# Latent attention in a two-layer encoder: shuffled rope halves, half-bank query sums, and scores of two heads in one chain

## The chip, the cores and the metric

The kernel runs on one core of one Trainium2 chip. The metric is device time in microseconds. The kernel before took 2838.72 us, the median of three runs (2837.63 to 2839.24). One core has a matrix engine (TensorE, PE in the views, with PEld for its weight loads), a vector engine (DVE), a scalar engine (ACT), GpSimd (POOL) and a queue that issues most transfers (SP). Each engine takes its instructions in the order in which they were written into its queue. PE writes its sums to PSUM, here eight banks of 128 partitions by 512 f32.

## The reference

The trunk has two layers, 256 tokens and 2048 features. Each layer mixes two attentions, then a gated feed-forward and a gated per-layer embedding follow. Cut to what matters here:

```
h  = rmsnorm(x, g_mix[i]);  z = h @ w_in[i]
dq, dk, dv, cq, ckv, kr, ga, gb = split(z)      # 8 heads of differential attention from dq, dk, dv
qf = (rmsnorm(cq) @ w_q_up[i]).reshape(b, s, 8, 128 + 64)
q_nope, q_rope = qf[..., :128], apply_rope(qf[..., 128:], cos_m, sin_m)
k_nope, v_mla  = split((rmsnorm(ckv) @ w_kv_up[i]).reshape(b, s, 8, 256), 2)
k_rope = apply_rope(kr)                         # one 64-wide rotary key for all 8 heads
scores = (q_nope . k_nope + q_rope . k_rope) * (128 + 64) ** -0.5
om     = softmax(scores) @ v_mla
m = sigmoid(ga) * (A @ w_branch_diff) + sigmoid(gb) * (om @ w_branch_mla);  x = x + m @ w_out[i]
```

apply_rope takes the two 32-wide halves x1, x2 of a 64-wide vector and gives [x1 c - x2 s, x2 c + x1 s].

## The kernel before

Activations lie feature by token: a tile is 128 features by 256 tokens. Every f32 operand of a product is cut into a high and a low part (`split`: ACT copies the high part, DVE subtracts it for the low one), and a product is high.high + high.low + low.high. Weights come by SP into `w` (four buffers), ACT makes `whi` and DVE makes `wlo` of each piece (three buffers each, lines 187 and 75). `product` and `pair` call `emit`: for each piece of 128 rows one matmul of `whi` with 512 columns (the high and low part of the activation side by side, L212) and one of `wlo` with the 256 high columns (L216). The two halves of the bank are then added by `joined`: ACT copies one half into `join`, DVE adds it to the other (`a<-mm,join`), into a scratch `a` that has four buffers. After that the bank is free. The pool `ps_mm` has four banks (`mm`, also `mmv` for the values), `ps_s` has two for scores (`S`), `ps_at` two for all else (`at`).

The order of each engine's queue is set by the framework's scheduler, which lays all instructions out on a modelled timeline; the program's order and the tile pools bound what it can do. A tile that takes a buffer over waits until all that used the buffer are done.

Per layer the stages follow each other so: values of the differential heads; the products for queries and keys of heads 0 to 7 (`queries_keys`), with `keys_up`, the narrow product of the rotary key and, at the end, `queries_up` laid beside the differential heads as filling (`beside`); the latent values (`vm`, L460 to L462 into `mmv`); the eight latent heads beside the 16 products of `gate(wga)`; the 16 products of `gate(wgb)`; the branch products, `w_out` and the feed-forward, which is most of the time.

Four things bear on the change. `queries_up(n)` makes two tiles of the 12 of `w_q_up`: n below 8 are the unrotated queries of heads n and n+1 (`qn`, written to `fa(n)`), n = 8 and 10 the rotated parts of four heads each (`qr`), which pass through `rotated`. `rotated` swaps the 32-wide halves by an f32 matmul with a permutation (`swap`, `swaps`, L367), multiplies by cosine and sine and splits the sum; for the rotary key it also copies the 64 rows to the other 64 (`halves`, L366) and fills two tiles `krs`, each zero on one half of its rows. `mla_weights(h)` makes one head's scores: two query blocks with six matmuls each, three of `qn` with `kn` and three of `qr` with one of `krs` over all 128 rows (L406); `exps` then takes the row maxima on DVE (L412) and the exponentials on ACT (L415). `mla_out(h)` transposes the weights and multiplies them with the values.

The tiles `fa0` to `fa7` have one buffer each. In a layer `fa(h)` first holds the key operand of differential head h, then its output `od[h]` (`diff_out`, L635), which `settle(0)` and `settle(4)` normalize four heads at a time: the squares' sums of the four heads go through `rsqrt` (eleven small DVE instructions, `rv`, `ry`, `ra`), the outputs are scaled (L81) and transposed (L647) into `ub` (ACT L251, DVE L78). `settle(4)` needs head 7. Only then can `fa(4)` to `fa(7)` take the latent queries of heads 4 to 7. The calls stand in the order

```python
            settle(0)
            for n in (8, 0, 2, 10):
                queries_up(n)
                yield
            settle(4)
            for n in (4, 6):
                queries_up(n)
```

Of the kernel before, what the change touches and what calls it, by code (L numbers as in the profile page):

```python
# [12 lines left out]
F32 = mybir.dt.float32  # L13
F32R = mybir.dt.float32r
# [5 lines left out]
P = 128  # L20
T = 256
# [32 lines left out]
def encoder(ctx, tc, x, p, positions, cols, lams, wq, wk, wv, wcq, wckv, wkr, wga, wgb,  # L54
# [16 lines left out]
    def bank(ps=ps_at, tag="at", name="at", shape=(P, 2 * T)):  # L71
        return ps.tile(list(shape), F32, tag=tag, name=name)

    def tt(o, a, b, op):
        return V.tensor_tensor(out=o, in0=a, in1=b, op=op)  # L75
# [43 lines left out]
    swap, swaps, halves = (rc[:, 4 + j * P : 4 + (j + 1) * P] for j in range(3))  # L119
    aside = [fa(j) for j in range(5)]  # L120
    posi = aside[0][:, 0, :].bitcast(I32)
    posf = aside[0][:, 1, :]
# [86 lines left out]
    def emit(acc, hi, lo, at, us, first, last, inside=None):  # L209
        for j, u in enumerate(us):  # L210
            s, start, stop = slice((at + j) * P, (at + j + 1) * P), first and j == 0, last and j == len(us) - 1
            lead = PE.matmul(acc, hi[:, s], u, start=start, stop=False)  # L212
# [27 lines left out]
    def joined(acc, o=None):  # L240
        t = scratch("join", 3)
        A.activation(t, acc[:, T:], AF.Copy)  # L242
        o = scratch("a", 4) if o is None else o
        tt(o, acc[:, :T], t, ALU.add)
        return o

    def split(u, src, gain=None):
        hi, lo = u[:, :T], u[:, T:]
        if gain is None:
            return A.activation(hi, src, AF.Copy), tt(lo, src, hi.bitcast(F32), ALU.subtract)  # L250
        return A.activation(hi, src, AF.Copy, scale=gain), stt(lo, src, gain, hi.bitcast(F32), ALU.mult, ALU.subtract)  # L251
# [104 lines left out]

    krs = [const.tile([P, 2 * T], F32R, name=f"kr{j}") for j in range(2)]
    for t in krs:  # L360
        nc.gpsimd.memset(t.bitcast(F32), 0.0)

    def rotated(a, c_, s_, o=None):
        r = bank()
        if o is None:
            PE.matmul(r[:, T:], halves, a, start=True, stop=True)  # L366
        PE.matmul(r[:, :T], swap if o is not None else swaps, a, start=True, stop=True)  # L367
        t = scratch("sh", 2)
        tt(t, r[:, :T], s_, ALU.mult)
        tt(a, a if o is not None else r[:, T:], c_, ALU.mult)  # L370
        tt(a, a, t, ALU.add)
        if o is None:
            for j, t in enumerate(krs):
                split(t[64 * j : 64 * j + 64], a[64 * j : 64 * j + 64])
        else:
            split(o, a)

# [20 lines left out]
    def scores(*maps):  # L398


        Ss = [bank(ps_s, "S", "S", (P, 2, T)) for _ in maps]
        for b in range(2):
            for j in range(len(maps[0])):
                for S, pairs in reversed(list(zip(Ss, maps))):
                    q, k = pairs[j]
                    PE.matmul(S[:, b, :], q[:, b * P : (b + 1) * P], k, start=j == 0, stop=j == len(pairs) - 1)  # L406
        return Ss
# [26 lines left out]

    def weights(tag="E", dt=F32):
        return tmp.tile([P, 2, T], dt, tag=tag, name=tag, bufs=2)

    last_exp = [None]
    ROPE16 = [(j + 8) if j < 8 else (j - 8) if j < 16 else j for j in range(32)]

    def values(src, us, load=None):
# [43 lines left out]
    for L in range(DEPTH):  # L485
# [64 lines left out]
                split(kn[-1], joined(acc))  # L550

        def queries_up(n):
            for acc in pair(w_q_up[L, n : n + 2], cq):
                if n < MH:
                    qn.append(operand(fa(len(qn), F32R)))
                    split(qn[-1], joined(acc))
                else:
                    if n > MH:
                        qr.append(operand(fc(len(qr) - 2, F32R)))
                    at = qr[len(qr) - 1] if n > MH else qr[ropes[0]]  # L560
                    rotated(joined(acc), cos_m, sin_m, at)
                    ropes[0] += 1

        ropes = [0]
# [102 lines left out]
        oms = ub[8:]  # L667
        todo = iter(range(NC))

        def mla_weights(h):  # L670
            E = weights()
            S, = scores(three(qn[h], kn[h]) + three(qr[h // 2], krs[h % 2]))
            r = exps(S, E, MLA_SCALE)
            for b in range(2):
                ts(E[:, b, :], E[:, b, :], r[:, b : b + 1], None, ALU.mult)
            return E

        def mla_out(h, W):
            v = head(vm, slice(None), h)
            vs = weights("E1", F32R)  # L680
            vh, vl = vs[:, :, :P], vs[:, :, P:]
            A.activation(vh, v, AF.Copy)
            tt(vl, v, vh.bitcast(F32), ALU.subtract)
            wh, wl = turned(W, True)
            yield
            o = bank()
            for kb in range(2):
                for j, (a, b) in enumerate(((vh, wh), (vh, wl), (vl, wh))):
                    PE.matmul(o[:, :T], a[:, kb, :], b[:, kb, :], start=kb + j == 0, stop=kb + j == 3)  # L689
# [196 lines left out]
        ("g_q_latent0", 4), ("g_q_latent1", 4), ("g_kv_latent0", 2), ("g_kv_latent1", 2), ("g_subln", 2)]  # L886


def rope_constants():


    c = np.zeros((P, 4 + 3 * P), np.float32)
    f32 = np.float32
    for base, dim in ((0, 16), (2, 64)):
        inv = f32(THETA) ** (-np.arange(0, dim, 2, dtype=f32) / f32(dim))
        for q in range(P):
            d = q % 64
            if d < dim:
                c[q, base] = inv[d % (dim // 2)]
                c[q, base + 1] = -1.0 if d < dim // 2 else 1.0  # L900
    for q in range(P):
        c[q, 4 + (q ^ 32)] = 1.0
        for m in (q, q ^ 64):
            c[q, 4 + P + (m ^ 32)] = 1.0
            c[q, 4 + 2 * P + m] = 1.0
    return c


# [18 lines left out]
def laid_out(a):  # L927
    a = {k: np.asarray(v) for k, v in a.items()}
    w_in = a["w_in"]
    cut = np.cumsum([0, 1024, 1024, 1024, QR, KVR, 64, DM, DM])  # L930
    z = [w_in[:, :, cut[j] : cut[j + 1]] for j in range(8)]
    up = a["w_q_up"].reshape(DEPTH, QR, MH, 192)
    kv = a["w_kv_up"].reshape(DEPTH, KVR, MH, 256)
    flat = lambda w: w.reshape(w.shape[0], w.shape[1], -1)
    named = {f"{n}{i}": a[n][i] for n in ("g_mix", "g_ffn", "g_ple", "g_q_latent", "g_kv_latent") for i in range(DEPTH)}
    named["g_final"] = a["g_final"]
    named["g_subln"] = a["g_subln"]
    return {
        "x": np.ascontiguousarray(a["x"][0].T.reshape(NC, P, T).transpose(1, 0, 2)),
        "p": np.ascontiguousarray(a["p"][:, 0].transpose(0, 2, 1).reshape(DEPTH, 2, P, T).transpose(0, 2, 1, 3)),  # L940
        "positions": np.ascontiguousarray(a["positions"]),
        "cols": np.ascontiguousarray(np.concatenate([columns(named[n]) for n, _ in COLS], axis=1)),
        "lams": np.ascontiguousarray(np.stack([a["lambda_q1"], a["lambda_q2"], a["lambda_k1"], a["lambda_k2"]], axis=1).reshape(1, -1)),
        "wq": tiles(z[0]), "wk": tiles(z[1]), "wv": wide(z[2]), "wcq": tiles(z[3]), "wckv": tiles(z[4]),
        "wkr": np.ascontiguousarray(z[5].reshape(DEPTH, NC, P, 64).transpose(0, 2, 1, 3)).reshape(DEPTH, P, NC * 64), "wga": tiles(z[6]), "wgb": tiles(z[7]),
        "w_q_up": tiles(np.concatenate([flat(up[..., :128]), flat(up[..., 128:])], axis=2)),
        "w_kn": tiles(flat(kv[..., :128])), "w_v": wide(flat(kv[..., 128:])),
        "w_bd": tiles(a["w_branch_diff"]), "w_bm": tiles(a["w_branch_mla"]), "w_out": tiles(a["w_out"]),
        "w_gate": tiles(a["w_gate_up"][:, :, :DFF]), "w_up": tiles(a["w_gate_up"][:, :, DFF:]),
        "w_down": tiles(a["w_down"]), "w_pin": tiles(a["w_ple_in"]), "w_pg": tiles(a["w_ple_gate"]),  # L950
        "rope_c": rope_constants(),
    }
# [17 lines left out]
```

## Time and profile before

| what | before |
|---|---|
| median of three runs | 2838.72 us |
| the profiled execution | 2838.84 us, its span 2837.0 us |
| granted TensorE clock, mean | 0.999 |
| busy: PE / PEld | 2826.8 us (100%) / 2498.5 us (88%) |
| busy: DVE / ACT | 2073.0 us (73%) / 1527.5 us (54%) |
| transfers | 531.49 MB, mean 187 GB/s |

Matmuls are pipelined, so their durations overlap: a row of the groups gives about 0.28 us for one of 256 columns, while the chain of work counts only the step from one end to the next. A PE that is 100% busy by the durations may therefore still wait for a fraction of a microsecond between two matmuls; such a wait is read from the steps.

### The profile page before, as it was taken

What the parts mean: (1) busy time and instruction counts of PE and PEld (TensorE: products, weight loads), DVE (VectorE), ACT (ScalarE), POOL (GpSimd) and SP (SyncE); (2) the same over time, 40 slices, a digit from 0 to 9 for tenths busy, and PEclk for the clock granted to TensorE, in tenths of its full rate; (3) what the DMA queues carried; (4) which work ended last, traced back from release to release, by engine and by line L of the source; (5) the groups of instructions that cost most, each with busy time, mean ns of one, the idle gap of its engine ahead of it and who ended that gap; (6) DMA issues with size and microseconds to landing.
All of it is one profiled execution on the core that took longest, in us unless ns stands there. A gap on an engine that the chain in (4) does not pass through costs nothing.

```text
span 2837.0 us, 44038 instructions
## 1 busy us (share of the span) xinstructions
PE 2826.8 (100%) x16743; PEld 2498.5 (88%) x16743; DVE 2073.0 (73%) x3537; ACT 1527.5 (54%) x2548; POOL 1.9 (0%) x15
## 2 busy tenths in 40 slices
PE   9999999999999999999999999999999999999998
PEld 7888888888888888888888888888888888888888
DVE  7997658776666766677869976687766666666777
ACT  6676545554444444455646755555544444444556
POOL 0000000000000000000000000000000000000000
PEclk9999999999999999999999999999999999999999
DMA  7544466666665566566665445666666656666664
GB/s 244 169 161 149 162 194 197 192 194 193 187 199 193 182 198 201 194 193 194 193 192 169 155 150 168 195 197 194 193 193 187 199 193 187 202 194 194 193 193 155
DMA packets 156596, 531.49 MB, mean 187 GB/s; under 512 B 16992, under 2 KB 24160, under 8 KB 156384
## 3 DMA queue, kind: packets, MB, share of 16 engines
q1 hardware_dynamic: 155952, 528.09, 58.9%
q8 instruction: 131, 2.15, 0.3%
q14 instruction: 81, 0.66, 0.1%
q10 hardware_dynamic: 432, 0.59, 0.1%
HBM read 526.52 MB, written 2.10 MB: 186 GB/s over the span
## 4 chain that ended last, share of the span: by engine, by line
PE 99%; DMA 1%; DVE 0%; ACT 0%; issue 0%; SPq 0%; DVEq 0%; ACTq 0%
PE mm L212 61%; PE mm L216 31%; PE S L406 1%; PE mmv L462 1%; PE mmv L460 1%; PE mmv L461 1%; DMA w<-in_wv 1%; PE at L424 1%; PE at L632 1%; PE at L689 0%; PE mm L776 0%; PE mm L392 0%; DVE wlo L75 0%; PE at L647 0%; DVE a L75 0%; PE at L367 0%
## 5 line engine op out<-in xcount | busy, mean ns | idle before, releaser
L187 ACT ACTIVATE whi<-w 128x1024 fp32r<-128x1024 f32 (+2 forms) x1030 | 1063.1, 1033 | 1241.4 <-issue 704.3
L75 DVE TENSOR_TENSOR wlo<-w,whi 128x1024 fp32r<-128x1024 f32 (+2 forms) x1030 | 1224.4, 1189 | 676.5 <-ACT whi L187 667.8
L212 PE MATMUL mm<-ub,whi 128*128 128x512 f32 x3936 | 1342.3, 390 | 0.3
L212 PE MATMUL mm<-ua,whi 128*128 128x512 f32 x3712 | 1271.4, 390 | 0.0
L216 PE MATMUL mm<-ub,wlo 128*128 128x256 f32 x3936 | 1085.1, 276 | 0.0
L216 PE MATMUL mm<-ua,wlo 128*128 128x256 f32 x3712 | 1027.3, 277 | 0.0
L212 PEld LDWEIGHTS mm<-ub,whi 128*128 128x128 f32 x3936 | 738.2, 188 | 153.1 <-DVE a L75 0.7
L212 PEld LDWEIGHTS mm<-ua,whi 128*128 128x128 f32 x3712 | 696.0, 188 | 142.0
L216 PEld LDWEIGHTS mm<-ub,wlo 128*128 128x128 f32 x3936 | 738.8, 188 | 1.1
L216 PEld LDWEIGHTS mm<-ua,wlo 128*128 128x128 f32 x3712 | 696.9, 188 | 2.4 <-DVE wlo L75 0.6
L75 DVE TENSOR_TENSOR a<-mm,join 128x256 f32<-128x256 f32 (+1 forms) x423 | 175.1, 416 | 1.6 <-ACT join L805 1.4
L242 ACT ACTIVATE join<-mm 128x256 f32<-128x256 f32 x452 | 166.5, 370 | 5.2 <-PE mm L216 4.8
L75 DVE TENSOR_TENSOR xT<-xT,mm 128x256 f32<-128x256 f32 x256 | 106.8, 420 | 41.5 <-PE mm L216 37.7
L75 DVE TENSOR_TENSOR a<-a,row 128x256 f32<-128x256 f32 (+1 forms) x209 | 87.5, 422 | 5.9
L75 DVE TENSOR_TENSOR a<-a 128x256 f32<-128x256 f32 x120 | 50.8, 425 | 4.0
L460 PE MATMUL mmv<-whi,ua 128*128 128x512 f32 x128 | 50.1, 395 | 1.7 <-ACT whi L187 1.7
L75 DVE TENSOR_TENSOR ua<-a,ua 128x256 fp32r<-128x256 f32 x120 | 49.9, 417 | 1.0 <-ACT ua L250 1.0
L461 PE MATMUL mmv<-whi,ua 128*128 128x512 f32 x128 | 49.6, 391 | 0.0
L250 ACT ACTIVATE ua<-a 128x256 fp32r<-128x256 f32 x120 | 48.2, 403 | 2.6 <-DVE a L75 2.6
L415 ACT ACTIVATE E<-S,nm 128x256 f32<-128x256 f32 x96 | 44.2, 472 | 2.1 <-DVE nm L81 2.0
L462 PE MATMUL mmv<-wlo,ua 128*128 128x512 f32 x128 | 43.8, 393 | 0.1
L75 DVE TENSOR_TENSOR ssq<-ssq,sq 128x256 f32<-128x256 f32 x96 | 40.1, 417 | 0.3 <-ACT sq L280 0.3
(195 smaller groups left out, 1209.8 us busy)
## 6 DMA issues: line engine op xcount, KB each, us to landing
w<-in_w_gate SPq DMA_DIRECT2D x176, 512.0 KB, 4.7
w<-in_w_up SPq DMA_DIRECT2D x176, 512.0 KB, 4.7
w<-in_w_down SPq DMA_DIRECT2D x128, 512.0 KB, 4.1
w<-in_wga SPq DMA_DIRECT2D x64, 512.0 KB, 3.8
w<-in_wgb SPq DMA_DIRECT2D x64, 512.0 KB, 4.1
w<-in_w_out SPq DMA_DIRECT2D x64, 512.0 KB, 4.6
w<-in_w_pg SPq DMA_DIRECT2D x64, 512.0 KB, 4.7
w<-in_w_down SPq DMA_DIRECT2D x64, 384.0 KB, 3.7
```

Source lines behind the costliest of these rows:

```text
L75: return V.tensor_tensor(out=o, in0=a, in1=b, op=op)
L187: last_split[:] = A.activation(hi[:, :m], w[:, :m], AF.Copy), tt(lo[:, :m], w[:, :m], hi[:, :m].bitcast(F32), ALU.subtract)
L212: lead = PE.matmul(acc, hi[:, s], u, start=start, stop=False)
L216: rest = PE.matmul(acc[:, T:], lo[:, s], u[:, :T], start=False, stop=stop)
L242: A.activation(t, acc[:, T:], AF.Copy)
L250: return A.activation(hi, src, AF.Copy), tt(lo, src, hi.bitcast(F32), ALU.subtract)
L406: PE.matmul(S[:, b, :], q[:, b * P : (b + 1) * P], k, start=j == 0, stop=j == len(pairs) - 1)
L415: last_exp[0] = A.activation(E[:, b, :], S[:, b, :], AF.Exp, bias=nm[:, b : b + 1], scale=scale, accum_out=sm[:, b : b + 1])
L424: PE.transpose(tp[:, kb, b * P : (b + 1) * P], W[:, b, kb * P : (kb + 1) * P], ident)
L460: PE.matmul(banks[half][b], xh, hi[:, s], start=a + j == 0, stop=False)
L461: PE.matmul(banks[half][b], xl, hi[:, s], start=False, stop=False)
L462: last_mm[:] = [PE.matmul(banks[half][b], xh, lo[:, s], start=False, stop=a + j == n - 1)]
```

## The change

The query sums of `queries_up` go into half a bank: three matmuls of 256 columns per 128 rows instead of one of 512 and one of 256, all added up in the same 256 columns. There is no `joined` any more: `split` and `rotated` read the bank itself. The rotated halves are stored shuffled by 16 (`LATENT_ORDER`, applied to the weights and tables before the launch), so that the swap of halves is a swap of neighbouring groups of 16 rows, which `stream_shuffle` on DVE does; the permutation matmuls L367 go, L366 for the key stays. There is one `kr` tile, full on both halves of its rows. `mla_weights(m)` makes the scores of heads 2m and 2m+1 in one chain of 24 matmuls, held in their order: 12 unrotated ones over 128 rows, then 12 rotated ones over 64 rows each, by turns on the lower half for one head and the upper half for the other. Both softmaxes follow. `mla_out` has a buffer of its own for the split values (`vs`).

```diff
-    def pair(src, us):
+    def pair(src, us, one=False):
...
             acc = bank(ps_mm, "mm", "mm")
-            emit(acc, hi, lo, j * n, us, True, True)
+            if one:
+                acc = acc[:, :T]
+                for k, u in enumerate(us):
+                    s = slice((j * n + k) * P, (j * n + k + 1) * P)
+                    for i, (w, x_) in enumerate(((hi, u[:, T:]), (hi, u[:, :T]), (lo, u[:, :T]))):
+                        PE.matmul(acc, w[:, s], x_, start=k + i == 0, stop=k + i == n + 1)
+            else:
+                emit(acc, hi, lo, j * n, us, True, True)
             yield acc
...
     def rotated(a, c_, s_, o=None):
-        r = bank()
         if o is None:
-            PE.matmul(r[:, T:], halves, a, start=True, stop=True)
-        PE.matmul(r[:, :T], swap if o is not None else swaps, a, start=True, stop=True)
+            r = bank()[:, :T]
+            PE.matmul(r, halves, a, start=True, stop=True)
+        else:
+            r, a = a, scratch("a", 4)
         t = scratch("sh", 2)
-        tt(t, r[:, :T], s_, ALU.mult)
-        tt(a, a if o is not None else r[:, T:], c_, ALU.mult)
+        V.stream_shuffle(t, r, SWAP16)
+        tt(t, t, s_, ALU.mult)
+        tt(a, r, c_, ALU.mult)
         tt(a, a, t, ALU.add)
...
-            for acc in pair(w_q_up[L, n : n + 2], cq):
+            for acc in pair(w_q_up[L, n : n + 2], cq, True):
                 if n < MH:
                     qn.append(operand(fa(len(qn), F32R)))
-                    split(qn[-1], joined(acc))
+                    split(qn[-1], acc)
...
-        def mla_weights(h):
-            E = weights()
-            S, = scores(three(qn[h], kn[h]) + three(qr[h // 2], krs[h % 2]))
...
+        def mla_weights(m):
+            hs = 2 * m, 2 * m + 1
+            Ss = [bank(ps_s, "S", "S", (P, 2, T)) for _ in hs]
+            terms = [(S, b, q, k) for S, h in zip(Ss, hs) for b in range(2) for q, k in three(qn[h], kn[h])]
+            rows = slice(0, 64), slice(64, P)
             for b in range(2):
-                ts(E[:, b, :], E[:, b, :], r[:, b : b + 1], None, ALU.mult)
-            return E
+                for pairs in zip(*(three(qr[m][r], kr[r]) for r in rows)):
+                    terms += [(S, b, q, k) for S, (q, k) in zip(Ss, pairs)]
+            done = []
+            for i, (S, b, q, k) in enumerate(terms):
+                with ExitStack() as stack:
+                    if done:
+                        stack.enter_context(tc.issue_after(done[-1].ins))
+                    done.append(PE.matmul(S[:, b, :], q[:, b * P : (b + 1) * P], k, start=i in (0, 6), stop=i > 21))
...
-        pipelined(mla_weights, mla_out, MH, lambda: gate(wga, gate_a, next(todo)))
+        nxt = mla_weights(0)
+        for m in range(MH // 2):
+            Ws = nxt
+            gate(wga, gate_a, next(todo))
+            nxt = mla_weights(m + 1) if m + 1 < MH // 2 else None
...
```

In the queues the change moves instructions at the passage from the differential heads to the latent ones, in both layers alike. The line numbers of the changed kernel are a few higher: L406 of the scores is L690 there for the latent heads, L424 (transposes of the weights) L430, L632 (weights by values) L639, L647 L654, and L460 to L462 are L467 to L469.

PE, where the latent scores start; `E` is a softmax, `vals,wt` the product of a differential head, `fa_2218` to `fa_2706` the outputs of heads 4 to 7, `mmv` the latent values. Before:

```order
L406 MATMUL S<-kr_135,ub_106 128x256 x2
L406 MATMUL S<-fb_1291,fa_2579 128x256 x3
L406 MATMUL S<-kr_135,ub_106 128x256 x3
L406 MATMUL S<-kr_136,ub_106 128x256 x2
L406 MATMUL S<-fb_1303,fa_2595 128x256 x3
L424 MATMUL at<-ident,E 128x128
L367 MATMUL at<-a,rc 128x256
L424 MATMUL at<-ident,E 128x128 x3
L406 MATMUL S<-kr_136,ub_106 128x256 x2
L460 MATMUL mmv<-whi,ub_104 128x512
L461 MATMUL mmv<-whi,ub_104 128x512
L462 MATMUL mmv<-wlo,ub_104 128x512
```

and in the changed kernel:

```order
L690 MATMUL S<-fb_1288,fa_2578 128x256 x6
L690 MATMUL S<-fb_1300,fa_2594 128x256 x6
L690 MATMUL S<-kr,ub_106 128x256 x12
L430 MATMUL at<-ident,E 128x128 x4
L690 MATMUL S<-fb_1483,fa_2625 128x256 x6
L690 MATMUL S<-fb_1495,fa_2641 128x256 x6
L690 MATMUL S<-kr,ub_107 128x256 x12
L639 MATMUL at<-vals,wt 128x128 x4
L654 MATMUL at<-ident,fa_2218 128x128 x2
L654 MATMUL at<-ident,fa_2421 128x128 x2
L690 MATMUL S<-fb_1678,fa_2771 128x256
L654 MATMUL at<-ident,fa_2602 128x128 x2
```

The first `mmv` matmul stood ahead of the last product of a differential head; now it stands behind it (the next row), and behind the scores of four latent heads and three pairs of transposes of `settle(4)`.

ACT, from the first exponentials of the latent heads; `fa_2711` before and `fa_2706` after are the output of differential head 7, `vals` the latent values, `fc` rotated queries. Before:

```order
L415 ACTIVATE E,sm<-S,nm 128x256 x2
L250 ACTIVATE fc_2671<-a 128x256
L187 ACTIVATE whi<-w_2926 128x1024
L635 ACTIVATE fa_2711<-at 128x256
L467 ACTIVATE vals<-mmv 128x512 x2
L637 ACTIVATE fa_2711,ssd<-fa_2711 128x128
L682 ACTIVATE E_2977<-vals 128x2x128
L682 ACTIVATE E_3123<-vals 128x2x128
L637 ACTIVATE fa_2711,ssd<-fa_2711 128x128
L415 ACTIVATE E,sm<-S,nm 128x256 x2
L250 ACTIVATE fc_2693<-a 128x256
L467 ACTIVATE vals<-mmv 128x512
```

and in the changed kernel:

```order
L187 ACTIVATE whi<-w_2923 128x1024
L257 ACTIVATE fc_2670<-a 128x256
L257 ACTIVATE fc_2692<-a 128x256
L629 ACTIVATE E<-E,rsum 128x256 x2
L421 ACTIVATE E,sm<-S,nm 128x256 x2
L421 ACTIVATE E_2910,sm<-S,nm 128x256 x2
L432 ACTIVATE wt<-at 128x512
L421 ACTIVATE E,sm<-S,nm 128x256 x2
L421 ACTIVATE E_3009,sm<-S,nm 128x256 x2
L642 ACTIVATE fa_2706<-at 128x256
L644 ACTIVATE fa_2706,ssd<-fa_2706 128x128 x2
L258 ACTIVATE ub_96<-at,gsub 128x256
```

The copy and the squares of head 7's output stood behind the exponentials of one latent head; now they stand behind those of four. `whi<-w_2923` is the first piece of the gate's weights.

DVE, at the end of `settle(4)`; `fa_2772` before and `fa_2771` after is the latent query of head 4, the others follow. Before:

```order
L81 TENSOR_SCALAR fa_2426<-fa_2426,ry 128x128 x2
L81 TENSOR_SCALAR fa_2607<-fa_2607,ry 128x128 x2
L81 TENSOR_SCALAR fa_2711<-fa_2711,ry 128x128 x2
L75 TENSOR_TENSOR wlo<-w_3050,whi 128x1024
L75 TENSOR_TENSOR wlo<-w_3072,whi 128x1024
L78 SCALAR_TENSOR_TENSOR ub_96<-at,gsub,ub_96 128x256
L75 TENSOR_TENSOR fa_2772<-a,fa_2772 128x256
L78 SCALAR_TENSOR_TENSOR ub_97<-at,gsub,ub_97 128x256
L75 TENSOR_TENSOR fa_2788<-a,fa_2788 128x256
```

and in the changed kernel:

```order
L81 TENSOR_SCALAR fa_2602<-fa_2602,ry 128x128 x2
L81 TENSOR_SCALAR fa_2706<-fa_2706,ry 128x128 x2
L78 SCALAR_TENSOR_TENSOR ub_96<-at,gsub,ub_96 128x256
L75 TENSOR_TENSOR fa_2771<-mm,fa_2771 128x256
L78 SCALAR_TENSOR_TENSOR ub_97<-at,gsub,ub_97 128x256
L75 TENSOR_TENSOR fa_2787<-mm,fa_2787 128x256
L78 SCALAR_TENSOR_TENSOR ub_98<-at,gsub,ub_98 128x256
L75 TENSOR_TENSOR fa_2809<-mm,fa_2809 128x256
L78 SCALAR_TENSOR_TENSOR ub_99<-at,gsub,ub_99 128x256
L75 TENSOR_TENSOR fa_2825<-mm,fa_2825 128x256
```

The queries of heads 4 to 7 are written at the same place, behind the transposes of `settle(4)`, but are now read from the banks `mm` and no more from the scratches `a`.

More of the change, by code (lines that the diff above doesn't have):

```diff
@@ L118, in encoder @@
         nc.gpsimd.memset(times[:, k : k + 1], 64.0 * 0.25 ** (k % 3) * (EPS if k > 2 else 1.0 / DM))
-    swap, swaps, halves = (rc[:, 4 + j * P : 4 + (j + 1) * P] for j in range(3))
+    halves = rc[:, 4 : 4 + P]
     aside = [fa(j) for j in range(5)]
@@ L355, in accumulate @@
         tt(xT[:, n, :], xT[:, n, :], acc[:, T:], ALU.add)
-    krs = [const.tile([P, 2 * T], F32R, name=f"kr{j}") for j in range(2)]
-    for t in krs:
-        nc.gpsimd.memset(t.bitcast(F32), 0.0)
+    kr = const.tile([P, 2 * T], F32R, name="kr")
     def rotated(a, c_, s_, o=None):
-        r = bank()
         if o is None:
-            PE.matmul(r[:, T:], halves, a, start=True, stop=True)
-        PE.matmul(r[:, :T], swap if o is not None else swaps, a, start=True, stop=True)
+            r = bank()[:, :T]
+            PE.matmul(r, halves, a, start=True, stop=True)
+        else:
+            r, a = a, scratch("a", 4)
         t = scratch("sh", 2)
-        tt(t, r[:, :T], s_, ALU.mult)
-        tt(a, a if o is not None else r[:, T:], c_, ALU.mult)
+        V.stream_shuffle(t, r, SWAP16)
+        tt(t, t, s_, ALU.mult)
+        tt(a, r, c_, ALU.mult)
         tt(a, a, t, ALU.add)
         if o is None:
-            for j, t in enumerate(krs):
-                split(t[64 * j : 64 * j + 64], a[64 * j : 64 * j + 64])
+            split(kr, a)
         else:
@@ L438, in encoder @@
     last_exp = [None]
+    SWAP16 = [(j + 16) % 32 for j in range(32)]
     ROPE16 = [(j + 8) if j < 8 else (j - 8) if j < 16 else j for j in range(32)]
@@ L560, in queries_up @@
                     at = qr[len(qr) - 1] if n > MH else qr[ropes[0]]
-                    rotated(joined(acc), cos_m, sin_m, at)
+                    rotated(acc, cos_m, sin_m, at)
                     ropes[0] += 1
@@ L668, in encoder @@
         todo = iter(range(NC))
-        def mla_weights(h):
-            E = weights()
-            S, = scores(three(qn[h], kn[h]) + three(qr[h // 2], krs[h % 2]))
-            r = exps(S, E, MLA_SCALE)
-            for b in range(2):
-                ts(E[:, b, :], E[:, b, :], r[:, b : b + 1], None, ALU.mult)
-            return E
+        def mla_weights(m):
[3 more added lines that the diff above has]
+            rows = slice(0, 64), slice(64, P)
+            for b in range(2):
+                for pairs in zip(*(three(qr[m][r], kr[r]) for r in rows)):
[6 more added lines that the diff above has]
+                    done.append(PE.matmul(S[:, b, :], q[:, b * P : (b + 1) * P], k, start=i in (0, 6), stop=i > 21))
+            got = []
+            for S, tag in zip(Ss, ("E", "E1")):
+                E = weights(tag)
+                r = exps(S, E, MLA_SCALE)
+                for b in range(2):
+                    ts(E[:, b, :], E[:, b, :], r[:, b : b + 1], None, ALU.mult)
+                got.append(E)
+            return got
         def mla_out(h, W):
             v = head(vm, slice(None), h)
-            vs = weights("E1", F32R)
+            vs = weights("vs", F32R)
             vh, vl = vs[:, :, :P], vs[:, :, P:]
@@ L690, in mla_out @@
             split(oms[h], o[:, :T])
-        pipelined(mla_weights, mla_out, MH, lambda: gate(wga, gate_a, next(todo)))
+        nxt = mla_weights(0)
[3 more added lines that the diff above has]
+            nxt = mla_weights(m + 1) if m + 1 < MH // 2 else None
+            for k, W in enumerate(Ws):
+                if k:
+                    gate(wga, gate_a, next(todo))
+                out_ = mla_out(2 * m + k, W)
+                next(out_)
+                gate(wga, gate_a, next(todo))
+                next(out_, None)
         for n in range(NC):
@@ L886 @@
         ("g_q_latent0", 4), ("g_q_latent1", 4), ("g_kv_latent0", 2), ("g_kv_latent1", 2), ("g_subln", 2)]
+LATENT_ORDER = [q // 32 * 16 + q % 16 + q % 32 // 16 * 32 for q in range(64)]
 def rope_constants():
-    c = np.zeros((P, 4 + 3 * P), np.float32)
+    c = np.zeros((P, 4 + P), np.float32)
     f32 = np.float32
@@ L896, in rope_constants @@
         for q in range(P):
-            d = q % 64
+            d = q % 64 if dim < 64 else LATENT_ORDER[q % 64]
             if d < dim:
@@ L901, in rope_constants @@
     for q in range(P):
[L902 removed]
         for m in (q, q ^ 64):
[L904 to L905 removed]
+            c[q, 4 + m] = 1.0
     return c
```

4 lines of the change are left out of this document (2 added, 2 removed).

## The prediction

> **What bounds the kernel now.** I read the page first, then what PE waits for, then the chain of work in order of time over the first layer's passage from differential to latent heads.
>
> ```profile
> span 2837.0 us, 44038 instructions
> PE 2826.8 (100%) x16743; PEld 2498.5 (88%) x16743; DVE 2073.0 (73%) x3537; ACT 1527.5 (54%) x2548; POOL 1.9 (0%) x15
> PE 99%; DMA 1%; DVE 0%; ACT 0%; issue 0%; SPq 0%; DVEq 0%; ACTq 0%
> PE mmv L460 <- ACT whi L187: 1.7, 1, 1.7
> ```
>
> The kernel is one row of matmuls: 99% of the chain is PE, and the one wait of PE above 1 us is 1.7 us at the start. So a matmul step removed is a step off the time, and every microsecond in which PE finds nothing ready is added in full: nothing later has slack to give it back. What the change does on DVE and ACT counts only where PE comes to wait for it. The steps, from the chain:
>
> ```profile
> 205.05 0.23 PE mm L212
> 205.39 0.23 PE mm L212
> 209.25 0.91 PE S L406 x12
> 210.16 0.43 PE mm L212
> 213.33 0.45 PE at L367 x2
> 228.40 0.89 PE at L632 x8
> 254.06 0.44 PE at L424 x4
> 277.71 1.43 PE S L406 x12
> 285.03 0.72 PE at L689 x6
> ```
>
> A pair of L212 and L216 takes 0.34 us (205.05 to 205.39). Twelve scores over 128 rows take 1.43, 0.12 each. Twelve over 64 rows by turns (the differential head at 209.25) take 0.91, and the next L212 has 0.43 where 0.23 is usual, so leaving them costs 0.20 more: 1.11.
>
> PE already waits once per layer in this passage, inside what the page calls busy:
>
> ```profile
> 217.52 0.59 PE L406 MATMUL S<-fb,fa 128*128 128x256 f32 x3
> 218.26 0.50 PE L212 MATMUL mm<-ub,whi 128*128 128x512 f32 x1
> ```
>
> From the end of one (218.11) to the end of the next (218.76) are 0.65 us, 0.42 above the usual 0.23. It ends when DVE frees an accumulator bank.
>
> **PE's own work.** The permutation matmuls go:
>
> ```profile
> L367 PE MATMUL at<-a,rc 128*128 128x256 f32 x20 | 5.9, 379 | 0.0
> L406 PE MATMUL S<-kr,ub 128*128 128x256 f32 x48 | 8.8, 284 | 0.0
> L406 PE MATMUL S<-kr,fc 128*128 128x256 f32 x48 | 8.4, 283 | 0.0
> ```
>
> All 20 of L367 leave, ten pairs at 0.44 (0.45 above): -4.4 us. The 96 rotated score matmuls took 96 x 0.12 = 11.4; they become eight chains of twelve at 1.11 = 8.9: -2.5 (no gain if turns on half rows came to nothing, -4.2 without the cost of leaving). The Trainium skill, TensorEngine Tiling (Array Packing), sections Theoretical Speedup and Key Properties, promises up to 2x for contractions of 64 rows and says that a change of tiling mode drains the engine. By its 2x alone the term would be -5.7; the row at 209.25 shows less, and the 0.20 behind it agrees with a drain.
>
> The half-bank sums add a matmul: 24 sums of four row blocks, each block three steps of 0.12 (0.72 for six at 285.03) instead of a pair of 0.34: 96 x 0.02 = +1.9, or nothing if the steps were as short as in a pair. In sum PE's work falls by 4.4 + 2.5 - 1.9 = 5.0 us, between 3 and 8.
>
> **DVE and ACT.** Without `joined`, 24 ACT copies and 24 DVE additions go. Eight additions are replaced by shuffles out of PSUM, which the trace has only out of SBUF, at about an addition's price; a few tenths more each would lie under DVE's lead over PE. The smaller table load and the key's two splits instead of four lie under other work too. All this I count as nothing, except that the wait of 0.42 goes: -0.8 for two layers.
>
> **What the edit takes away with the copies.** The scratches `a` were also a store. These are the queries of heads 4 to 7 before:
>
> ```profile
> 221.85 0.74 DVE L75 TENSOR_TENSOR a<-mm,join 128x256 f32<-128x256 f32 x2
> 224.93 0.39 PE L460 MATMUL mmv<-whi,ub 128*128 128x512 f32 x1
> 242.24 0.22 PE at L647 x2
> 244.54 0.41 DVE L75 TENSOR_TENSOR fa<-a,fa 128x256 fp32r<-128x256 f32 x1
> 251.19 0.41 DVE L75 TENSOR_TENSOR fa<-a,fa 128x256 fp32r<-128x256 f32 x1
> ```
>
> Their sums left the banks by 222.6, the latent values started at 224.93, and the queries reached `fa` only at 244.5 to 251.6, behind the transposes of `settle(4)`. Meanwhile PE did 12 value matmuls and then gate products. In the changed kernel the four sums stay in the four `mm` banks until `settle(4)` is through: neither values nor gates can start, and PE has only the scores of heads 0 to 3 left. Those need the two `S` banks twice, so the second chain waits for the first one's exponentials, and head 7's last product, on which `settle(4)` depends, stands behind it in PE's queue. The prices of the links:
>
> ```profile
> 197.62 1.28 DVE L412 TENSOR_REDUCE nm<-S 128x2 f32<-128x512 f32 x2
> 200.29 0.23 DVE L81 TENSOR_SCALAR nm<-nm 128x2 f32<-128x2 f32 x2
> 200.71 0.47 ACT L415 ACTIVATE E<-S,nm 128x256 f32<-128x256 f32 x1
> 202.41 0.22 ACT L415 ACTIVATION_READ_ACCUMULATOR E<-S,nm 128x1 f32 x1
> 203.39 0.95 ACT L622 ACTIVATE E<-E,rsum 128x256 f32<-128x256 f32 x2
> 204.48 1.09 ACT L187 ACTIVATE whi<-w 128x1024 fp32r<-128x1024 f32 x1
> 204.59 0.87 DVE L78 SCALAR_TENSOR_TENSOR E<-E,rsum,E 128x256 f32<-128x256 f32 x2
> 207.75 1.22 DVE L75 TENSOR_TENSOR wlo<-w,whi 128x1024 fp32r<-128x1024 f32 x1
> 221.09 0.39 ACT L635 ACTIVATE fa<-at 128x256 f32<-128x256 f32 x1
> 222.16 0.18 ACT L637 ACTIVATION_READ_ACCUMULATOR fa<-fa 128x1 f32 x1
> 235.90 0.17 DVE L78 SCALAR_TENSOR_TENSOR ry<-ra,ry 128x8 f32<-128x8 f32 x1
> 236.50 0.17 DVE L78 SCALAR_TENSOR_TENSOR ry<-ra,ry 128x8 f32<-128x8 f32 x1
> 238.39 1.65 DVE L81 TENSOR_SCALAR fa<-fa,ry 128x128 f32<-128x128 f32 x8
> 242.87 0.46 ACT L251 ACTIVATE ub<-at,gsub 128x256 fp32r<-128x256 f32 x1
> 243.23 0.41 ACT L250 ACTIVATE fa<-a 128x256 fp32r<-128x256 f32 x1
> 244.15 0.48 DVE L78 SCALAR_TENSOR_TENSOR ub<-at,gsub,ub 128x256 fp32r<-128x256 f32 x1
> ```
>
> So four exponentials take 1.92 (200.71 to 202.63), an output's copy and squares 1.25 (221.09 to 222.34), a small step of `rsqrt` 0.20 (three from 235.90 to 236.50), a pair of scales 0.42 (1.65 / 4).
>
> *First gap.* Let a be the end of the last query matmul on PE. Head 7's scores end about 8.5 us before: a query sum of 1.44 and transposes of 0.44, two sums, a product of 0.89, two sums. In that time ACT first waits for the buffer of the second value piece (free after 4.9), then splits it (1.09), copies and squares head 6's output (1.25) and makes head 7's exponentials (1.92): it is done at about a + 0.6. Then, in the queue's order, the gate's first piece on ACT (1.09), two rotated queries (0.4 each, 0.75 by their steps) and the scaling of head 7 (0.95) to a + 3.3; on DVE the piece's low part (1.22 from a + 1.65, to 2.9), two rotated queries (0.75), half the weighted difference (0.4), the maxima of heads 0 and 1 (1.28), the other half (0.4): a + 5.7. Only then head 7's weights can be transposed. PE ran out at a + 2.5 (1.43 + 1.11): 3.2 us idle. The exponentials of heads 0 and 1 run from a + 5.9, behind two small steps of 0.23, to 7.85; the first frees its `S` bank at 6.9, the other at 7.85. PE has transposed by 6.15, waits 0.75, does six scores, and waits 0.25 more. In all 4.2 us per layer.
>
> *Second gap.* Let t be the end of the chain of heads 2 and 3. Maxima and one small step 1.44; four exponentials 1.92; copy and squares of head 7 1.25; eleven steps of `rsqrt` 2.2; the first scales 0.42; two transposes, 0.38 with their run-out; high parts on ACT 0.77 (242.87 to 243.64); low parts on DVE 0.80 (244.15 to 244.95). With about 0.1 for hand-overs it is 9.3 us to the first free `mm` bank. PE has 0.89 of head 7's product and 0.6 of transposes and one score matmul in it: 7.8 us idle. After that the other three banks come free every 0.8 us or so, faster than PE uses them (six value matmuls of 0.23).
>
> Two layers: 2 x (4.2 + 7.8) = +24.0 us.
>
> **The clock after a gap.** The first 16 matmuls of the kernel against the same form later:
>
> ```profile
> 1.05 3.78 PE L476 MATMUL at<-ones 128*128 128x128 f32 x16 [1.05 <-DVE ones L115]
> ```
>
> 3.78 us for 16 is 0.236 each; L632 above takes 0.89 / 8 = 0.11. So PE starts at about half speed and loses some 1.9 us in its first 3.8. Whether it falls back in mid-kernel no row shows; the 7.8 us gap is nearer to a start than to a fraction of a microsecond, so I take 1.9 once a layer, +3.8 in all, with bounds of 0 and 7.6 (both gaps). The Trainium skill, TensorE: Matmul & The Clock Gate, Part 1, has the clock at half after an idle window of about 3.4 us, and full after a busy one; by it the long gap counts surely and the first one perhaps. The slow first matmuls agree, a return to half speed no run here shows.
>
> **Sum.** -5.0 - 0.8 + 24.0 + 3.8 = +22.0. The profiled execution took 2838.84, 0.1 above the median of 2838.72: 2860.7 us.
>
> **Rivals.** *The clock stays up* (15%): the same gaps at full speed, 2860.7 - 3.8 = 2856.9. For it: no row shows a fall; against it the start.
>
> *Only the second gap* (15%): if head 7's weights are ready when the first chain ends, because ACT takes its exponentials before the second value piece or DVE runs further ahead, 2 x 7.8 - 5.8 = +9.8, and 0 to 3.8 for the clock: 2848.4 to 2852.2.
>
> *Longer gaps* (15%): each link is queued behind others on two engines, and a sixth more per link with half speed after both gaps gives 27.6 + 7.6 - 5.8 = +29.4: 2868.
>
> *Faster* (8%): PE finds its matmuls ready, as before, since ACT and DVE have less to do; then -5.8 alone, 2833.0. It decides for a gain when both gaps together stay below 2.9 us a layer. Against it: the release of the banks needs head 7's whole chain, and the orders put it last. That the half-row turns or the half-bank sums don't do what they say would move the sum by 2 to 3 us and is in the ranges.
>
> **Numbers.** My forecast as told has 45%; the four rivals above 15, 15, 15 and 8; 2 are left for what I don't see. 8 in 10 lies from 2846 (only the long gap, a little shorter) to 2871 (the longer gaps, a little more). A measurement of this kernel can tell about 0.2%, 5.7 us. The gain case sits on that edge: half of it counts as faster with part of the rest, 0.05, the other half as same, 0.04; slower 0.91.
>
> **What would show it.** Right: PE busy well below 100%, with two new waits per layer in the list of PE's waits, at transposes of `E` behind DVE and at the latent values behind DVE, the last some 8 us; the two layers alike; L367 gone; twelve-chains of 0.91 at L690; a granted clock below 0.999. Wrong: latent values that start within 2 us of the last query sum, or a span shorter than before.

## The result, and the profile after

The changed kernel took 2859.61 us (median of six runs, 2858.67 to 2861.14), the kernel before 2838.83 us beside it: 1.0075 of it, 95% interval 1.0062 to 1.0088. The page and PE's waits after (us in total, times, the longest):

```profile
span 2857.8 us, 44134 instructions
PE 2829.9 (99%) x16819; PEld 2501.5 (88%) x16819; DVE 2070.4 (72%) x3531; ACT 1520.5 (53%) x2522; POOL 1.0 (0%) x13
PE 97%; ACT 1%; DMA 1%; DVE 1%; issue 0%; SPq 0%; DVEq 0%; ACTq 0%
PE at L654 <- DVE fa L81: 11.9, 2, 6.2
PE at L430 <- DVE E L78: 5.1, 4, 1.4
PE at L483 <- DVE ones L115: 1.1, 1, 1.1
PE S L690 <- ACT E L421: 0.9, 2, 0.6
PE S L690 <- ACT fa L257: 0.8, 2, 0.4
```

But for the one at the start (L483), the waits come in the same places of the two layers, 18.8 us in all by the timeline, on an engine that waited in none of these places before. The passage of layer 0 on PE's timeline (start, duration, operation; idle before it in brackets):

```profile
219.60 1.59 PE L690 MATMUL S<-fb,fa 128*128 128x256 f32 x12
221.13 0.98 PE L690 MATMUL S<-kr,ub 64*128 64x256 f32 x12
223.47 0.30 PE L430 MATMUL at<-ident,E 128*128 128x128 f32 x1 [1.37 <-DVE E L78]
224.97 0.55 PE L430 MATMUL at<-ident,E 128*128 128x128 f32 x3 [1.20 <-DVE E L78]
226.16 2.56 PE L690 MATMUL S<-fb,fa 128*128 128x256 f32 x12 [0.65 <-ACT E L421]
228.65 1.65 PE L690 MATMUL S<-kr,ub 64*128 64x256 f32 x12
230.23 1.16 PE L639 MATMUL at<-vals,wt 128*128 128x128 f32 x8
237.56 1.09 PE L654 MATMUL at<-ident,fa 128*128 128x128 f32 x4 [6.16 <-DVE fa L81]
239.06 0.58 PE L690 MATMUL S<-fb,fa 128*128 128x256 f32 x1 [0.41 <-ACT fa L257]
239.72 0.78 PE L467 MATMUL mmv<-whi,ub 128*128 128x512 f32 x1
240.29 0.63 PE L468 MATMUL mmv<-whi,ub 128*128 128x512 f32 x1
244.27 0.40 PE L468 MATMUL mmv<-whi,ub 128*128 128x512 f32 x1
```

The first chain of 24 takes 2.5 us and ends at 222.11. Then come the two gaps, 1.37 + 1.20 + 0.65 and 6.16 + 0.41, 9.8 us; layer 1 has the other 9.0. The second thing to see is the durations: the same 24 scores take 4.1 us from 226.16, and a value matmul at 240.29 takes 0.63 where the one at 244.27 takes 0.40. The granted clock of these stretches (columns: the stretch, its length, PE, PEld, DVE, ACT and POOL busy with counts, PEclk, DMA share, GB/s):

```profile
222.20:225.60 3.40, 0.84 (x4) 0.45 (x4) 2.87 (x9) 0.71 (x4) 0.00 (x0) 1.00 0.56 193
226.10:230.30 4.20, 4.13 (x25) 3.58 (x25) 1.57 (x6) 1.42 (x6) 0.00 (x0) 0.59 0.01 4
237.50:243.90 6.40, 5.93 (x20) 4.91 (x21) 3.62 (x13) 2.73 (x7) 0.00 (x0) 0.50 0.01 3
244.00:250.00 6.00, 6.00 (x34) 5.13 (x33) 3.25 (x6) 5.14 (x10) 0.00 (x0) 1.00 0.19 54
```

The first value matmul starts 0.1 us after DVE has moved the first of the four held queries out of its bank (239.58). The next two banks come free 0.7 and 1.1 us later, the fourth only at 245.56, but PE does not wait for them:

```profile
238.25 0.47 ACT L258 ACTIVATE ub<-at,gsub 128x256 fp32r<-128x256 f32 x1 [3.38 <-PE at L654]
239.16 0.42 DVE L75 TENSOR_TENSOR fa<-mm,fa 128x256 fp32r<-128x256 f32 x1
```

For the experiments I cut PE's steps into stretches by the same instructions in every trace, from one matmul's end to another's: the *passage* runs from the last L216 of the latent projections (199.5 us before) to the last L216 of the second gate (425.8 before). All other stretches of the two layers agree between all kernels here to 0.1 us, except the one ahead of it, which is 0.43 us a layer shorter wherever the key is shuffled (its permutation matmul, two steps of 0.216), and the start, which varies by 0.3 to 1.3 us. What follows the last matmul varies by up to 0.6 us.

| kernel | median, us | ratio to before, interval | passage, layers 0 / 1, us |
|---|---|---|---|
| before | 2838.14 to 2838.83 | 1 | 226.3 / 226.3 |
| changed | 2859.61 | 1.0075, 1.0062 to 1.0088 | 237.9 / 236.7 |
| copies out of the banks | 2831.82 | 0.9976, 0.9967 to 0.9985 | 223.3 / 223.3 |
| joined sums | 2835.79 | 0.9991, 0.9981 to 1.0 | 225.6 / 225.6 |
| single heads | 2857.56 | 1.0067, 1.0052 to 1.0082 | 234.3 / 237.7 |
| warm gap | 2856.94 | 1.0067, 1.005 to 1.0084 | 236.3 / 235.6 |
| late queries | 2856.56 | 1.0062, 1.0047 to 1.0077 | 234.9 / 236.3 |
| shuffles alone | 2837.56 | 0.9997, 0.9987 to 1.0006 | 226.4 / 226.5 |
| copies, single heads | 2835.28 | 0.9989, 0.9979 to 0.9998 | 225.1 / 225.1 |
| mixed sums | 2832.37 | 0.9978, 0.9969 to 0.9987 | 223.5 / 223.5 |

### The profile page after: what moved, and what is told of

It reads as the page before. It is cut to its first block, busy times and chain, and to the rows that moved or that the text cites. A ratio compares the mean times of both kernels' runs of the same rounds, so it can differ in the third digit from the quotient of the medians.

```text
span 2857.8 us, 44134 instructions
## 1 busy us (share of the span) xinstructions
PE 2829.9 (99%) x16819; PEld 2501.5 (88%) x16819; DVE 2070.4 (72%) x3531; ACT 1520.5 (53%) x2522; POOL 1.0 (0%) x13
## 4 chain that ended last, share of the span: by engine, by line
PE 97%; ACT 1%; DMA 1%; DVE 1%; issue 0%; SPq 0%; DVEq 0%; ACTq 0%
PE mm L212 60%; PE mm L216 30%; PE mm L242 1%; PE mmv L469 1%; PE mmv L467 1%; PE mmv L468 1%; PE S L690 1%; PE at L430 1%; PE S L412 1%; DMA w<-in_wv 0%; PE at L639 0%; PE at L711 0%; PE mm L809 0%; DMA xT<-in_x 0%; ACT E L421 0%
## 5 line engine op out<-in xcount | busy, mean ns | idle before, releaser
L212 PE MATMUL mm<-ub,whi 128*128 128x512 f32 x3840 | 1307.0, 389 | 0.0
L212 PE MATMUL mm<-ua,whi 128*128 128x512 f32 x3712 | 1271.3, 390 | 0.0
L216 PE MATMUL mm<-ub,wlo 128*128 128x256 f32 x3840 | 1058.4, 276 | 0.0
L216 PE MATMUL mm<-ua,wlo 128*128 128x256 f32 x3712 | 1026.6, 277 | 0.0
L212 PEld LDWEIGHTS mm<-ub,whi 128*128 128x128 f32 x3840 | 720.1, 188 | 148.3
L212 PEld LDWEIGHTS mm<-ua,whi 128*128 128x128 f32 x3712 | 696.1, 188 | 142.3
L216 PEld LDWEIGHTS mm<-ub,wlo 128*128 128x128 f32 x3840 | 720.7, 188 | 1.0
L216 PEld LDWEIGHTS mm<-ua,wlo 128*128 128x128 f32 x3712 | 697.0, 188 | 1.5
L75 DVE TENSOR_TENSOR a<-mm,join 128x256 f32<-128x256 f32 x399 | 166.2, 418 | 1.5 <-ACT join L838 1.4
L249 ACT ACTIVATE join<-mm 128x256 f32<-128x256 f32 x428 | 156.7, 367 | 3.1 <-PE mm L216 2.8
L467 PE MATMUL mmv<-whi,ua 128*128 128x512 f32 x128 | 50.2, 396 | 0.8 <-ACT whi L187 0.7
L469 PE MATMUL mmv<-wlo,ua 128*128 128x512 f32 x128 | 44.0, 394 | 0.1
```

The lines of the kernel that those rows point to most:

```text
L467: PE.matmul(banks[half][b], xh, hi[:, s], start=a + j == 0, stop=False)
L469: last_mm[:] = [PE.matmul(banks[half][b], xh, lo[:, s], start=False, stop=a + j == n - 1)]
```

## The experiments

Two theories of the gaps stood against each other. *Held banks*: the query sums of heads 4 to 7 sit in all four `mm` banks until `settle(4)` frees `fa(4)` to `fa(7)`. *The score chain*: the 24 scores of heads 2 and 3 stand ahead of head 7's product in PE's queue and wait for the `S` banks.

### The hold taken away by copies

```diff
                 if n < MH:
                     qn.append(operand(fa(len(qn), F32R)))
+                    if n >= 4:
+                        o = scratch("a", 4)
+                        A.activation(o, acc, AF.Copy)
+                        acc = o
                     split(qn[-1], acc)
```

> The changed kernel, with one edit: ACT copies the sums of latent heads 4 to 7 from their banks into the scratches a, and the splits read those. Theory of the held banks: the latent values find free banks ahead of head 7's chain, the second gap of about 6 us a layer goes, the first one (3.2 us a layer) may stay in part; 2838.8 - 5.8 + 0 to 6.4 = 2833 to 2840 us, granted clock 0.999 if no gap over 3 us is left. Rival, the chain of 24 scores that stands ahead of head 7's product and needs both S banks twice is the cause by itself: a gap of 5 us or more a layer stays, 2848 us or more.

2831.82 us, 0.9976 of before: slightly under the range of held banks, and 28 us below the changed kernel for eight ACT copies more, four a layer. PE's only wait over 1 us is at the start; between the two score chains there are now the values:

```profile
PE at L483 <- DVE ones L115: 1.1, 1, 1.1
...
223.68 0.98 PE L694 MATMUL S<-kr,ub 64*128 64x256 f32 x12
224.59 0.33 PE L430 MATMUL at<-ident,E 128*128 128x128 f32 x1
224.68 0.47 PE L467 MATMUL mmv<-whi,ub 128*128 128x512 f32 x1
...
205.00:245.00 40.00, 40.00 (x293) 36.45 (x292) 34.65 (x90) 29.21 (x76) 0.00 (x0) 1.00 0.42 142
```

Both gaps are gone, with both score chains still there. The first gap goes because the values fill it, not because head 7's weights are ready sooner. With every edit the scheduler lays the queues anew, so these runs show the hold together with the order that it leads to; no run keeps the order and changes the hold alone.

### Whole-bank sums again, the rest of the change kept

```diff
-            for acc in pair(w_q_up[L, n : n + 2], cq, True):
+            for acc in pair(w_q_up[L, n : n + 2], cq):
...
-                    split(qn[-1], acc)
+                    split(qn[-1], joined(acc))
...
-                    rotated(acc, cos_m, sin_m, at)
+                    rotated(joined(acc), cos_m, sin_m, at)
```

> The changed kernel with whole-bank sums and joined for all query products, as before; shuffles and score chains of two heads stay. Held banks: no gap, 2838.8 - 4.4 - 2.5 = 2832 us, up to 2835 with short waits. Rival, the score chain: gaps as in the changed kernel, 2848 us or more.

2835.79 us: no gap, so again held banks, but 1 us above the upper end. PE waits instead for the additions of `joined`:

```profile
PE mm L212 <- DVE a L75: 3.7, 4, 1.2
```

In PE's steps it is 2.4 us a layer: 0.95 and 1.47 beyond the usual 0.23 ahead of two L212 of the query products.

### Single heads, the half-bank sums kept

```diff
-        def mla_weights(m):
...
+        def mla_weights(h):
+            E = weights()
+            S, = scores(three(qn[h], kn[h]) + three(qr[h // 2], krs[h % 2]))
...
+        pipelined(mla_weights, mla_out, MH, lambda: gate(wga, gate_a, next(todo)))
```

> The changed kernel with the scores of one head at a time over 128 rows and the two zero-padded key tiles of before; shuffles and half-bank sums stay. Held banks: the values still wait for settle(4), a gap of 4 to 9 us a layer, 2848 to 2862 us. Rival, the score chain: the gaps go, 2838.8 - 4.4 + 1.9 = 2836 us.

2857.56 us, in the range of held banks: without any two-head chain almost the whole loss is there. PE's waits, sums over both layers:

```profile
PE at L657 <- DVE fa L81: 6.2, 2, 3.1
PE at L433 <- DVE E L78: 2.6, 2, 1.3
PE at L657 <- DVE ub L78: 1.5, 2, 0.8
PE at L642 <- ACT wt L435: 1.4, 2, 0.7
```

The gap behind head 7's product is 3.1 us instead of 6.2, since only two softmaxes stand ahead of the settling there instead of four. So the score chains do take part, in the length of the gaps; by themselves they make none (the two runs above).

This run also shows the clock by itself. Its layers have the same instructions and, to 0.2 us, the same waits, and yet the passage takes 234.3 us in one and 237.7 in the other:

```profile
223.30:245.00 21.70, 15.39 (x82) 12.70 (x82) 15.15 (x51) 11.87 (x34) 0.00 (x0) 0.92 0.15 47
1640.50:1667.50 27.00, 22.17 (x101) 18.69 (x102) 15.94 (x49) 13.19 (x36) 0.00 (x0) 0.75 0.15 48
```

In layer 1 the clock fell after the first gap too, in layer 0 only after the second; the last section shows where the two differ.

### The second gap filled

```diff
+            if h0:
+                w, i = bank()[:, :T], last_out[0]
+                for _ in range(FILL):
+                    with tc.issue_after(i.ins):
+                        i = PE.matmul(w, ones_r, ua[0][:, :T], start=True, stop=True)
             rd = rsqrt(ssd[:, 2 * h0 : 2 * h0 + 8], P, SUB_EPS, 8)
```

> The changed kernel with 44 matmuls of 256 columns of no use behind head 7's product, in the second gap (5.3 us at full speed, in a gap of 6.2), so that PE is not idle there. If the slow steps behind the gap are the clock's fall after idleness, the matmuls behind it take full-speed steps (value matmuls 0.23 instead of 0.43), PE's granted clock rises above 0.995 and the time falls by 2 to 5 us against the changed kernel: 2855 to 2858. If the slow steps have another cause, or the filling delays head 7's chain: 2859.6 us or more.

2856.94 us. The medians are 2.7 us apart, but the intervals of the ratios overlap; the passages, which leave the start out, are 1.7 and 1.1 us shorter. Behind the filled gap PE is at full speed, behind the unfilled first one it is not:

```profile
231.50 5.46 PE L653 MATMUL at<-ua,ones 128*128 128x256 f32 x44
...
239.77 0.40 PE L469 MATMUL mmv<-whi,ub 128*128 128x512 f32 x1
...
225.60:230.00 4.40, 4.36 (x24) 4.00 (x24) 1.56 (x6) 1.39 (x5) 0.00 (x0) 0.50 0.02 4
239.40:246.00 6.60, 6.60 (x38) 5.69 (x37) 4.02 (x9) 4.87 (x10) 0.00 (x0) 1.00 0.00 1
```

So the slow steps behind the long gap come from PE having been idle. The trace counts 18.1 us of PE work at half clock in both layers of the changed kernel and 9.8 here, so by half of that the slow steps cost 4.1 us less. Of this 1.3 are lost again: the filling and the steps around it take that much more than the 10.8 us of idle time that go. Behind the first gap of layer 0 the clock even stays at half for longer than in the changed kernel, from 224.34 to 231.17.

### The queries of heads 4 to 7 behind the values

```diff
             settle(4)
-            for n in (4, 6):
-                queries_up(n)
...
         vm, = (v for v in values(w_v[L], ckv) if v is not None)
+        for n in (4, 6):
+            queries_up(n)
```

> The changed kernel with the query products of heads 4 to 7 placed behind the latent values in the program; nothing is added. Held banks: the values run early, and 48 query matmuls (5.7 us) fill most of the wait for settle(4) behind head 7's product; the first gap stays. PE's work 5.8 us less than before, waits of 2 to 5 us a layer, some loss to the clock: 2836 to 2846 us. If only removing the hold altogether helps: as the changed kernel, 2857 us or more.

2856.56 us: a miss by 10.6 us. The values do run first (their last ends at 219.7), and then hold the banks in their turn: `vals` has one buffer, which head 7's product still reads, and the queries wait for it, with a further wait of 4.0 us at the transposes of `settle(4)` in one layer. In all PE waits 6.6 and 8.7 us in the two passages, where 2 to 5 were expected, and the clock falls again.

```profile
PE at L430 <- DVE E L78: 5.3, 4, 1.4
PE mm L242 <- ACT vals L474: 4.1, 2, 3.2
PE at L652 <- DVE fa L81: 4.0, 1, 4.0
```

So here too sums wait in the banks for head 7, only other ones.

### The shuffles alone

```diff
-        PE.matmul(r[:, :T], swap if o is not None else swaps, a, start=True, stop=True)
+        V.stream_shuffle(t, r, SWAP16)
```

> The kernel before with the shuffled halves alone: whole-bank sums with joined, scores of one head over 128 rows. The permutation matmuls leave, 20 steps of 0.216 us: 2838.1 - 4.3 = 2833.8 us if nothing waits. If the shortage is DVE's work between the query sums (joined's additions hold the banks, as in the run with joined sums), PE waits 1 to 2.5 us a layer for banks: 2836 to 2838 us.

2837.56 us, 0.9997 of before (0.9987 to 1.0006): the 4.3 us of permutation matmuls leave PE, and most of it comes back as waiting for banks: the passages, which lose 1.7 us of them a layer, are no shorter than before. `joined` frees the bank on DVE, and DVE now also has the shuffles while PE reaches the next sum sooner.

```profile
PE mm L212 <- DVE a L75: 3.3, 6, 1.1
```

### Copies and single heads

The edits of the copies and of the single heads together.

> The run with the copies out of the banks, with the scores of one head at a time over 128 rows as before. It gives the worth of the two-head chains where nothing waits: by the steps 0.33 us for each of eight chains, so 2831.8 + 2.6 = 2834.4 us. If the chains cost as much in waits as they save: 2832 us or less.

2835.28 us, 3.5 us above the copies alone: the two-head chains are worth 1.8 us a layer by the passages (225.1 against 223.3). The steps explain 1.3; a wait of 0.59 for a bank that the single heads have and the chains do not (in PE's steps at a query sum) is the rest. The four kernels with and without the hold and the chains also price the hold: 27.8 us with the chains (2859.61 against 2831.82), 22.3 without them (2857.56 against 2835.28).

### Mixed sums

```diff
-            for acc in pair(w_q_up[L, n : n + 2], cq, True):
+            for acc in pair(w_q_up[L, n : n + 2], cq, n not in (4, 6)):
...
-                    split(qn[-1], acc)
+                    split(qn[-1], joined(acc) if n >= 4 else acc)
```

> The changed kernel with whole-bank sums and joined for heads 4 to 7 alone. The hold goes as with the copies; 32 sums of a row block a kernel cost a pair (0.34) instead of three steps (0.357), 0.5 us less, but DVE adds eight additions more while it is the shorter engine, and one rotated chain stands broken in the queue, which costs another 0.2 to 0.4 a layer: 2830.5 to 2834 us, no gap over 1 us.

2832.37 us, not told apart from the copies (the intervals overlap, the passages are 0.2 us longer). Either way of taking the four sums out of the banks gives a kernel 0.2% faster than before, with both intervals below 1. Between the two the passages alone speak for the copies.

## Why the prediction was right, and where its terms were not

The forecast of 2860.7 us is 1.1 us from the measured 2859.61, and the mechanism is shown: the half-bank sums lose their store, the four banks wait for head 7, and copies alone turn +20.8 us into -6.3. But two terms were mis-sized, one against the other, and that the sum came out so close is luck: the gaps were 5.2 us shorter than forecast, and the clock cost 5.2 more.

*The gaps*: forecast 24.0 us, measured 18.8. In the first one I had 4.2 us a layer where 3.2 and 2.9 were: ACT came to the gate's first piece 0.3 us earlier, one of the four transposes went ahead with half the weights, and I added several durations whose steps overlap. In the second one the links came out: 9.3 us forecast from the end of the scores (230.30) to the first free bank, 9.3 measured (239.58). Only the idle part of it is 6.6 and 6.2 in the two layers instead of 7.8, since PE's own work in it took longer: in layer 0 head 7's product 1.09 with its run-out for 0.89, and the transposes and the score matmul, at half clock, 1.75 for 0.6. That the banks behind the first come free every 0.8 us was wrong for the fourth (4.1 us behind the third).

*The clock*: forecast 3.8 us, one fall a layer. It fell after both gaps, in both layers. The passage of the changed kernel is 11.6 us longer than before in layer 0; PE's work and the old waits give -3.0 (the copies' run, which has no gap), the waits 9.8, so 4.8 are left for slow steps, and by the same sum 4.4 in layer 1. The trace's record of the clock gives the same: PE worked 9.4 and 8.7 us at half clock, half of which is 4.7 and 4.3, some 9.0 us, above my bound of 7.6 as well. The bound was wrong because it priced one slow start, 3.8 us long and 1.9 us dear, per gap. In layer 0 PE worked at half clock for 6.0 us behind the second gap, in layer 1 for 5.6 behind the first.

*PE's work and the waits*: forecast -5.0 - 0.8 = -5.8, measured -6.8 where nothing waits (twice 3.0 + 0.43). The permutations are 4.3 for the forecast 4.4, the chains 1.3 a layer by their steps as forecast, the half-bank sums cost 0.7 a layer instead of 0.95. A wait of 0.26 a layer near the end of the latent heads, which I had not seen in the trace of before (its chain has it at 332.45, 0.38 where a step of L216 is 0.11), left with the change:

```profile
332.45 0.38 PE mm L216
```

*DVE's share* I counted as nothing. That was right for the shuffles' own price (0.452 us out of PSUM, 0.446 out of SBUF) and wrong as a reading of the half-bank sums: I booked them as a loss of 1.9 us on PE, while, beside the shuffles and the chains, dropping the additions of `joined` is worth 4 us (2835.79 against 2831.82), because DVE frees the banks there.

The rivals: the clock that stays up is refuted by the granted clock, only the second gap by the waits. Of the longer gaps the half speed after both gaps came, the length did not; a sixth more on 24.0 would also be 28.0 and not 27.6. The gain of 5.8 us is near what the kernel does once the hold is gone (6.3), so its price was about right and its condition was not met.

Of the signs, the waits at the transposes of `E`, the chains of 0.91, the missing permutations and the lower clock (0.995) came. Two did not: PE is still 99% busy, since 18.8 us are 0.7% of the span, and the long wait, 6.2 us and not 8, ends at the transposes of `settle(4)`, which stand ahead of the values in PE's queue.

## What to carry to other kernels

A scratch between an accumulator bank and its destination is also a store: before removing the copy that fills it, ask when the destination's buffer comes free, and who needs the bank meanwhile. On an engine without idle time the order of its queue shows what it will wait for; adding up the links from the old trace then gave the way to the first free bank to 0.1 us. The idle time in it also needs the work that the engine still does on that way, and was forecast a quarter too long. And where the engine's clock depends on its being busy, a gap costs more than its length.

## What the runs showed of the hardware

PE's granted clock fell to 0.50 after idle stretches of 1.37, 1.20 and 0.65 us with four transposes between them, none longer than 1.4 us. Behind the 6.2 us gap of layer 0 it stayed there for the next 6.4 us, behind the 5.8 us gap of layer 1 for 3.5.

The traces also show when it changes. Within a trace all changes behind the start lie whole multiples of 3.41 us apart; in the changed kernel they come at 226.86, 230.27, 233.69 and 243.93 in layer 0 and at 1643.39, 1650.22, 1653.63 and 1660.46 in layer 1. The stretches between (columns as above; the last two are of the single heads):

```profile
223.46:226.85 3.39, 1.53 (x9) 1.11 (x10) 2.28 (x8) 1.76 (x8) 0.00 (x0) 1.00 0.43 150
226.87:230.26 3.39, 3.39 (x22) 2.83 (x20) 0.88 (x4) 0.65 (x3) 0.00 (x0) 0.50 0.00 0
230.28:233.67 3.39, 1.11 (x10) 0.92 (x8) 2.27 (x7) 1.87 (x9) 0.00 (x0) 1.00 0.00 0
233.70:243.92 10.22, 5.95 (x21) 4.92 (x22) 6.61 (x28) 3.85 (x13) 0.00 (x0) 0.50 0.01 2
1639.99:1643.38 3.39, 1.76 (x18) 1.27 (x16) 3.00 (x6) 1.76 (x5) 0.00 (x0) 1.00 0.58 176
1643.40:1650.21 6.81, 5.60 (x28) 4.75 (x29) 2.74 (x11) 2.42 (x9) 0.00 (x0) 0.50 0.17 61
1653.64:1660.45 6.81, 3.06 (x10) 2.42 (x11) 6.12 (x29) 2.68 (x9) 0.00 (x0) 0.50 0.00 1
...
221.76:225.15 3.39, 1.94 (x15) 1.55 (x13) 3.16 (x7) 1.94 (x8) 0.00 (x0) 1.00 0.46 138
1638.29:1641.68 3.39, 1.70 (x12) 1.30 (x12) 3.39 (x10) 1.33 (x5) 0.00 (x0) 1.00 0.44 150
```

In the ten traces, cut along this grid, half clock followed on 13 of the 14 stretches at full clock in which PE was busy for 1.77 us or less, and on none in which it was busy for 1.89 or more. So no whole stretch need be idle, but the one exception (1.54 us busy, in the late queries) says that busy time alone is not all of it. The two layers of the single heads have the same waits, but the grid cuts them differently: 1.94 us busy in the stretch of layer 0, after which the clock stayed up, 1.70 in that of layer 1, after which it fell. The Trainium skill, TensorE: Matmul & The Clock Gate, Part 1, tells of a free-running window, by which the phase would matter; the spacing of 3.41 us and these two layers agree, but no run here moves the phase alone. The rule that the prediction cites from the Trainium skill, half clock after an idle window, asks for too much idle time: in these traces a half-idle one was enough in all cases but one.
